# FFN 0's gate and up-projection by seven products of block sums in place of eight of blocks

## The chip, the cores and the metric

The kernel runs on one core of one Trainium2 chip. The metric is the device time of one execution in microseconds (us), taken as the median of several runs. Beside it stands one profiled execution, from which every row of the profile comes.

## The reference

Two layers work on 512 latent tokens and 256 context tokens of width 1024. Each layer is a mixer (layer 0: grouped-query attention, layer 1: a bidirectional Mamba-2 scan) and a gated feed-forward network (FFN) with a width-3 convolution over positions on its gate:

```python
def conv_ffn(h, w_up, conv_w, conv_b, w_down):
    g, u = jnp.split(h @ w_up, 2, axis=-1)     # h (.., 1024), w_up (1024, 2 x 2816)
    g = dwconv_centred(g, conv_w, conv_b)      # over positions, width 3
    return (jax.nn.silu(g) * u) @ w_down       # w_down (2816, 1024)
```

In layer 0 this runs for both streams, 512 + 256 tokens, with the same weights. The input `h` is the RMS-normed stream with a scale and a shift, and the result enters the stream through a gate; scale, shift and gate are linear maps of SiLU of the condition vectors (the "modulation"). All is in f32.

## The kernel before

Activations lie transposed: features on the 128 partitions, tokens along the free axis. The 1024 input features are eight K tiles, the 2816 hidden features are 22 tiles f = 0 to 21. Every f32 operand of a large product is split into two fp32r parts, high and low (`split`: ScalarE casts the high part, VectorE, here DVE, subtracts for the low part, L85 and L87), and each product is three matmuls: weight high by activation high (L105), weight high by activation low (L106), weight low by activation high (L108). All three come from `mm3`.

FFN 0 is `ffn(g, 0, ...)`. For each f, `up(f)` computes the gate's tile with `gemm(f)` and the up tile with `gemm(22 + f)`. A `gemm` loads one weight tile of 128 x 1024 (`load_w`: a DMA on SyncE's queue into `wst`, then the split into `wh` and `wl`; all of these are tiles of the ring `t4`, ten buffers), and runs, for the latent stream with 512 columns and then for the context stream with 256, eight K tiles by three matmuls into one PSUM tile of two banks (`S`, two buffers). From the gate's PSUM, ScalarE makes `cv` (L833), DVE adds the two neighbouring taps (L837 and L838, for each stream), ScalarE applies SiLU (L839). DVE multiplies it with the up tile's PSUM into `hd` (L848), and `split` makes `hdh` and `hdl`. These are tiles of the ring `t3`, here 24 buffers.

The down-projection comes in flushes of two f each (`flush`, the first and the last of three): for each of the eight output tiles m, `down` accumulates the f's of the flush for both streams in two PSUM banks (four buffers of one bank), and DVE adds the result to the residual stream X (L784, once with 512 and once with 256 columns). The flush of a group is recorded after the first `up` of the next group.

Between these steps FFN 0 carries the modulation of layer 1 and of its own output gate: `ada_dve` is a generator that `up` and `down` advance (`next(side)`), two or more steps for each f and one for each m of a flush. A step is one DVE multiply-and-sum of a 128 x 1024 tile (`junk`, L167) on a weight tile `wada` that is loaded on SyncE's queue. The first 24 tiles serve two steps, the last 32 one. The ring of `wada` has three buffers:

```python
w = g.t3p.tile([P, D], F32, tag="wada", bufs=3, name="wada")
nc.sync.dma_start(w, g.I["adaT"][(ch + 1 if layer else 0) * KT + m])
```

A scheduler orders the instructions of each engine when the program is built, by the data they need, the free buffers and a model of durations; on the chip every engine and SyncE's DMA queue run in that order. The steps of `ada_dve` are held in program order.

The high and low parts of h are separate tiles for each stream (`htiles`, 16 of 512 and 16 of 256 columns).

Of the kernel before, what the change touches and what calls it, by code (L numbers as in the profile page):

```python
# [15 lines left out]
D = 1024  # L16
KT = D // P
L = 512
C = 256
T = L + C  # L20
# [4 lines left out]
NFT = FF // P  # L25
# [54 lines left out]

def split(g, src, hi, lo, lo_engine="dve", pin=False):

    nc = g.nc
    keep = g.tc.keep_in_program_order if pin else lambda i: i
    keep(nc.scalar.copy(hi, src))  # L85
    eng = nc.vector if lo_engine == "dve" else nc.gpsimd
    keep(eng.tensor_tensor(lo, src, _r(hi), ALU.subtract))  # L87
# [12 lines left out]
def mm3(g, w, outs, first, last):  # L100

    wh, wl = w
    mm = g.nc.tensor.matmul
    for out, (ah, al) in outs:
        mm(out, wh, ah, start=first, stop=False)  # L105
        mm(out, wh, al, start=False, stop=False)  # L106
    for out, (ah, al) in outs:
        mm(out, wl, ah, start=False, stop=last)  # L108
# [44 lines left out]
def ada_dve(g):  # L153


    nc = g.nc
    cb = g.t3p.tile([P, 2 * D], F32, name="cb")
    nc.sync.dma_start(cb, g.I["cflat"].broadcast_to([P, 2 * D]))
    follow(g, nc.scalar.activation(cb, cb, AF.Silu))
    for layer, ch, nv in [(0, 5, 2)] + [(1, ch, 2 if ch < 2 else 1) for ch in range(6)]:  # L160
        md = g.mod[layer][ch]
        for m in range(KT):
            w = g.t3p.tile([P, D], F32, tag="wada", bufs=3, name="wada")
            nc.sync.dma_start(w, g.I["adaT"][(ch + 1 if layer else 0) * KT + m])
            for v in range(nv):
                junk = g.t3p.tile([P, D], F32, tag="junk", bufs=1, name="junk")
                g.tc.keep_in_program_order(nc.vector.scalar_tensor_tensor(  # L167
                    junk, w, 1.0, cb[:, v * D : (v + 1) * D], ALU.mult, ALU.mult, accum_out=md[:, m, v : v + 1]))
                yield
        modulation(g, md[:, :, :nv], layer, ch, 0, KT, nv)  # L170
# [5 lines left out]
class Fill:  # L176
# [6 lines left out]
    def add(self, gen):  # L183
        self.q.append(gen)
# [83 lines left out]
    return out  # L268


def htiles(g, n, name):
    return tuple(g.p.tile([P, n], F32R, tag=f"h{n}", bufs=16, name=f"{p}{name}") for p in ("hh", "hl"))


def modulated(g, hl, x, rs, a, b, layer, ca, cb, v, m, pool=False):
# [26 lines left out]
def S(g, name):  # L302
    return g.ps.tile([P, 1024], F32, tag="S", bufs=2, name=name)
# [6 lines left out]
class Norm:  # L310
# [2 lines left out]

    def __init__(self, g, layer, ca, cb, streams, name):
        self.g, self.a, self.name, self.streams = g, (layer, ca, cb), name, streams
        self.h = [[htiles(g, n, f"{name}{i}_{m}") for m in range(KT)] for i, (n, v) in enumerate(streams)]
        self.acc = {}

    def sq(self, seg, x, m):
# [59 lines left out]
def attention(g, fill, X, late):  # L379


    nc, I = g.nc, g.I
    S64 = slice(0, 64), slice(64, 128)
    Bk, Sb = (lambda name: Bank(g, name)), (lambda name: S(g, name))
    t2 = lambda name, dt=F32: g.t3p.tile([P, 512], dt, tag="t2", bufs=6, name=name)
    g.h = [[htiles(g, n, f"a{i}_{m}") for m in range(KT)] for i, n in enumerate((L, C))]
    hl, hc = g.h
    kn = g.par[:, PC["kn"] : PC["kn"] + 1]

# [28 lines left out]
    xs = [[X[:, m, c0:c1] for m in range(KT)] for c0, c1 in ((0, L), (L, T))]  # L418
# [23 lines left out]
    norm = rstd_rows(g, acc, L, g.ones[:, :1], D, "a", Bk)  # L442
# [3 lines left out]
    e = g.p.tile([P, 2 * KT], F32, name="silu")  # L446
# [8 lines left out]
    rsl, _, _ = next(norm)  # L455
# [12 lines left out]
    for m in range(KT):  # L468
# [37 lines left out]
    raw = [t3(g, f"raw{j}") for j in range(6)]  # L506
# [207 lines left out]
    odram = [g.dp.tile([P, T], F32, name=f"odram{p}") for p in range(6)]  # L714

    def osplit(p):
        hl_, hc_ = htiles(g, L, f"ol{p}"), htiles(g, C, f"oc{p}")
# [13 lines left out]
    m = pairs[0].maxima()  # L731
# [8 lines left out]
    for p in range(NH // 2):  # L740
        m = iter(())
        if p < 7:
# [3 lines left out]
            m = pairs[p + 1].maxima()  # L746
# [49 lines left out]
def ffn(g, layer, streams, x, h, first, nxt=None, side=iter(()), after=()):  # L796

    nc, I = g.nc, g.I  # L800
    ns = len(streams)
    tot = sum(n for n, _ in streams)
    off = [0, L]

    cw = [g.par[:, PC[f"fw{layer}{t}"] : PC[f"fw{layer}{t}"] + NFT] for t in range(3)]
    cb = g.par[:, PC[f"fb{layer}"] : PC[f"fb{layer}"] + NFT]
    whole = [[(i, 0, n) for i, (n, _) in enumerate(streams)]]

    def gemm(t):

        if t % NFT == 0:
            ps = first[t // NFT]
        else:
            w = load_w(g, I["wup"][layer, t])
            if t % NFT == 1:
                out = []
                for i in range(ns):
                    ps = Bank(g, "ps_up1")
                    for _ in gemm_in(g, [(ps, w)], h, (0, 0), [[s] for s in whole[0] if s[0] == i]):
                        pass  # L820
                    out.append((ps, [i]))
                return [(ps[:, : streams[i][0]], off[i], off[i] + streams[i][0], i) for ps, (i,) in out]
            ps = S(g, "ps_up")
            for _ in gemm_in(g, [(ps, w)], h, off, [[s] for s in whole[0]]):
                pass
        return [(ps[:, :tot], 0, tot, None)]

    def up(f):
        pg = gemm(f)
        cv = t3(g, "cv", n=tot)  # L830
        w0, w1, w2 = (c[:, f : f + 1] for c in cw)
        for ps, a, b, _ in pg:
            nc.scalar.activation(cv[:, a:b], ps, AF.Identity, scale=w1, bias=cb[:, f : f + 1])  # L833
        for i in range(ns):
            a, b = off[i], off[i] + streams[i][0]
            ps, o = next((ps, o) for ps, o, e, j in pg if j in (None, i))
            nc.vector.scalar_tensor_tensor(cv[:, a + 1 : b], ps[:, a - o : b - o - 1], w0, cv[:, a + 1 : b], ALU.mult, ALU.add)  # L837
            nc.vector.scalar_tensor_tensor(cv[:, a : b - 1], ps[:, a - o + 1 : b - o], w2, cv[:, a : b - 1], ALU.mult, ALU.add)  # L838
# [4 lines left out]
        pu = gemm(NFT + f)  # L843
        for _ in range(some):
            next(side, None)
        hd = t3(g, "hd", n=tot)
# [32 lines left out]
def ssd(g, x, norm, wf, bg, close):  # L879


    nc, I, tc = g.nc, g.I, g.tc
    par = lambda name, j, rows=P: g.par[:rows, PC[name] + j : PC[name] + j + 1]
    h = norm.h
# [285 lines left out]
        prev = cur  # L1170


    xn = [[g.p.tile([P, C], F32, tag="h256", bufs=16, name=f"x{m}{i}") for i in range(2)] for m in range(KT)]
# [81 lines left out]
def body(nc, tc, I, out, dbg=None):  # L1255
# [3 lines left out]
    es = ExitStack()  # L1259
    pool = lambda n, st=es, **k: st.enter_context(tc.tile_pool(name=n, bufs=1, **k))  # L1260
    g.const, g.p = pool("const"), pool("p")
    g.ps = g.t3p = None
    phx, pha = ExitStack(), ExitStack()
    X = pool("x", phx).tile([P, KT, T], F32, name="X")
# [49 lines left out]
    first = first_tiles(g, wf, nrm, bg)  # L1314
    pha.close()
    phf = ExitStack()
    g.t3p, g.n3 = pool("pf", phf), 24


    def dump():  # L1320
# [13 lines left out]
        phf.close()  # L1334
        phx.close()

    x, nrm, first = ssd(g, x, nxt, wf, bg, close)
    phf = ExitStack()
    g.t3p, g.n3 = pool("pg", phf), 24
    if not (dbg and dbg.get("stage") == 3):  # L1340
# [105 lines left out]
```

## Time and profile before

| | |
|---|---|
| median of 3 runs | 1908.88 us (1906.4 to 1910.08) |
| profiled execution | 1914.7 us, its span 1912.9 us |
| mean granted TensorE clock | 0.994 |
| TensorE matmuls (PE) | 1876.5 us busy, 98% of the span |
| weight loads (PEld) | 1547.6 us, 81% |
| DVE | 1311.2 us, 69% |
| ScalarE (ACT) | 823.0 us, 43% |
| GpSimd (POOL) | 309.8 us, 16% |
| FFN 0's matmuls | about 418 to 1000 us of the span |

A row of a group names line, engine, operation, output and inputs with their shapes and the count; then the busy time in us and the mean ns of one; then the engine's idle time just ahead of these instructions and what ended it. A row of the timeline begins with the start and the length in us. Matmuls overlap: the time that one costs is the distance from its start to the next one's start, not its length. DVE's instructions overlap a little too.

### The profile page before, as it was taken

What the parts mean: (1) busy time and instruction counts of PE and PEld (TensorE: products, weight loads), DVE (VectorE), ACT (ScalarE), POOL (GpSimd) and SP (SyncE); (2) the same over time, 40 slices, a digit from 0 to 9 for tenths busy, and PEclk for the clock granted to TensorE, in tenths of its full rate; (3) what the DMA queues carried; (4) which work ended last, traced back from release to release, by engine and by line L of the source; (5) the groups of instructions that cost most, each with busy time, mean ns of one, the idle gap of its engine ahead of it and who ended that gap; (6) DMA issues with size and microseconds to landing.
All of it is one profiled execution on the core that took longest, in us unless ns stands there. A gap on an engine that the chain in (4) does not pass through costs nothing.

```text
span 1912.9 us, 27512 instructions
## 1 busy us (share of the span) xinstructions
PE 1876.5 (98%) x10834; PEld 1547.6 (81%) x10834; DVE 1311.2 (69%) x1943; ACT 823.0 (43%) x1426; POOL 309.8 (16%) x274
## 2 busy tenths in 40 slices
PE   9999999999999999999999999999999999999999
PEld 7866555678888888888888888888888878888887
DVE  5578778678877777444488777777888466565555
ACT  3634444255122222222266777776667352323331
POOL 2241111031000000000040344443434210000000
PEclk9989998999999999999999999999999999999999
DMA  9221332114434555221122443334443322323232
GB/s 337 78 89 45 113 112 95 34 45 166 132 122 132 174 188 166 66 67 60 62 89 87 121 118 115 126 113 133 120 138 115 91 77 86 102 88 110 88 100 88
DMA packets 73425, 210.02 MB, mean 110 GB/s; under 512 B 8912, under 2 KB 14416, under 8 KB 73168
## 3 DMA queue, kind: packets, MB, share of 16 engines
q1 hardware_dynamic: 73296, 208.26, 34.3%
q8 instruction: 85, 1.39, 0.3%
q14 instruction: 44, 0.36, 0.1%
HBM read 198.79 MB, written 6.82 MB: 107 GB/s over the span
## 4 chain that ended last, share of the span: by engine, by line
PE 79%; DVE 9%; issue 3%; ACT 2%; POOL 1%; DMA 1%; DVEq 0%; SPq 0%; POOLq 0%; ACTq 0%
PE ps_up L106 10%; PE ps_up L108 10%; PE ps_up L105 10%; PE ps_d L105 6%; PE ps_d L106 6%; PE ps_d L108 6%; PE ps_in L106 4%; PE ps_in L108 4%; PE ps_in L105 4%; PE ps_o L637 2%; PE ps_s L673 2%; PE ps_st L1033 2%; DVE ht L281 1%; PE ps_wo L108 1%; PE ps_wo L105 1%
## 5 line engine op out<-in xcount | busy, mean ns | idle before, releaser
L87 DVE TENSOR_TENSOR wl<-wst,wh 128x1024 fp32r<-128x1024 f32 x205 | 254.5, 1242 | 244.9 <-PE ps_up L106 137.7
L85 ACT CAST wh<-wst 128x1024 fp32r<-128x1024 f32 x211 | 221.2, 1049 | 423.2 <-DMA wst<-in_wup 333.8
L106 PE MATMUL ps_up<-hlf,wh 128*128 128x512 f32 x1008 | 357.0, 354 | 0.0
L105 PE MATMUL ps_up<-hhf,wh 128*128 128x512 f32 x1008 | 356.9, 354 | 0.0
L108 PE MATMUL ps_up<-hhf,wl 128*128 128x512 f32 x1008 | 356.8, 354 | 0.0
L105 PEld LDWEIGHTS ps_up<-hhf,wh 128*128 128x128 f32 x1008 | 190.5, 189 | 26.5
L106 PEld LDWEIGHTS ps_up<-hlf,wh 128*128 128x128 f32 x1008 | 190.6, 189 | 26.4
L108 PEld LDWEIGHTS ps_up<-hhf,wl 128*128 128x128 f32 x1008 | 190.5, 189 | 26.4
L105 PE MATMUL ps_in<-hhs,wh 128*128 128x512 f32 (+1 forms) x560 | 204.4, 365 | 0.0
L106 PE MATMUL ps_in<-hls,wh 128*128 128x512 f32 (+1 forms) x560 | 199.4, 356 | 0.0
L108 PE MATMUL ps_in<-hhs,wl 128*128 128x512 f32 (+1 forms) x560 | 198.7, 355 | 0.0
L105 PE MATMUL ps_d<-hdh,wh 128*128 128x512 f32 (+1 forms) x568 | 193.6, 343 | 1.4 <-DVE X L784 1.2
L108 PE MATMUL ps_d<-hdh,wl 128*128 128x512 f32 (+1 forms) x568 | 193.5, 341 | 0.0
L106 PE MATMUL ps_d<-hdl,wh 128*128 128x512 f32 (+1 forms) x568 | 193.0, 340 | 0.3 <-DVE hdl L87 0.3
L784 DVE SCALAR_TENSOR_TENSOR X<-ps_d,mod,X 128x512 f32<-128x512 f32 (+1 forms) x224 | 124.6, 583 | 36.9 <-PE ps_d L108 36.6
L106 PEld LDWEIGHTS ps_d<-hdl,wh 128*128 128x128 f32 x568 | 106.6, 188 | 14.8 <-DVE hdl L87 0.7
L105 PEld LDWEIGHTS ps_d<-hdh,wh 128*128 128x128 f32 x568 | 106.3, 188 | 14.8 <-DVE X L784 1.4
L105 PEld LDWEIGHTS ps_in<-hhs,wh 128*128 128x128 f32 x560 | 105.9, 189 | 15.1 <-issue 1.2
L108 PEld LDWEIGHTS ps_in<-hhs,wl 128*128 128x128 f32 x560 | 105.8, 189 | 14.8
L108 PEld LDWEIGHTS ps_d<-hdh,wl 128*128 128x128 f32 x568 | 106.7, 188 | 13.1
L106 PEld LDWEIGHTS ps_in<-hls,wh 128*128 128x128 f32 x560 | 106.0, 189 | 13.2
L676 ACT ACTIVATE pr<-ps_s 128x1024 f32<-128x1024 f32 x56 | 57.2, 1021 | 110.6 <-PE ps_s L675 109.6
(340 smaller groups left out, 3547.3 us busy)
## 6 DMA issues: line engine op xcount, KB each, us to landing
wst<-in_wup SPq DMA_DIRECT2D x88, 512.0 KB, 3.6
wada<-in_adaT SPq DMA_DIRECT2D x56, 512.0 KB, 3.9
wst<-in_win SPq DMA_DIRECT2D x48, 512.0 KB, 3.7
wst<-in_wdown SPq DMA_DIRECT2D x44, 512.0 KB, 3.6
E<-ad SPq DMA_DIRECT2D x64, 256.0 KB, 6.8
wada<-in_adaB SPq DMA_DIRECT2D x24, 512.0 KB, 4.6
ec<-ead SPq DMA_DIRECT2D x64, 128.0 KB, 5.0
wst<-in_wout SPq DMA_DIRECT2D x16, 512.0 KB, 3.6
```

The lines of the kernel that those rows point to most:

```text
L85: keep(nc.scalar.copy(hi, src))
L87: keep(eng.tensor_tensor(lo, src, _r(hi), ALU.subtract))
L105: mm(out, wh, ah, start=first, stop=False)
L106: mm(out, wh, al, start=False, stop=False)
L108: mm(out, wl, ah, start=False, stop=last)
L281: nc.vector.scalar_tensor_tensor(t[:, c0:c1], ap, g.moda[layer][ca][:, m, v : v + 1], rs[:, c0:c1], ALU.mult, ALU.mult)
L637: nc.tensor.matmul(po[S64[e], :n], v, pr[:, 512 * e + off : 512 * e + off + n], start=first, stop=last)
L673: nc.tensor.matmul(outs[e], a[S64[e], k], b[S64[e], q], start=i == 0, stop=False)
L676: nc.scalar.activation(pr, ps, AF.Exp)
L784: nc.vector.scalar_tensor_tensor(ap, o[:, c0:c1], gate[:, m, v : v + 1], ap, ALU.mult, ALU.add)
L1033: nc.tensor.matmul(ps[:, d * 256 : (d + 1) * 256], Bt[:, t * P : (t + 1) * P], xw[d][t], start=t == ts[0], stop=t == ts[-1])
```

## The change

Only the tiles f = 4 to 21 of FFN 0 and K tiles 0 to 3 of their eight are computed in another way. Take the product of weights (gate and up, that is two output blocks; two K blocks of two K tiles each) and activations (the same K blocks; two halves of 384 tokens of the 768): two by two blocks by two by two blocks. The eight products of blocks become seven products of sums of blocks, the scheme of Strassen in Winograd's form, with K tiles 4 to 7 added as before:

- `sums()`, once, ahead of f = 2: 20 adds and subtractions of 128 x 384 on GpSimd make four sums T0 to T3 of the activations, and four splits follow.
- `both(f)` takes the place of `gemm(f)` and `gemm(22 + f)`. It loads both weight tiles, makes four sums of 128 x 256 of the weights on GpSimd (`wss`), and splits gate (1024 columns), sums (1024) and the second to fourth quarter of up (768). Then come the products, each of 384 columns; `a` and `e` are the two banks of the first PSUM tile, `b` and `r` those of the second.
- The results are combined outside PSUM: four ScalarE copies (`p1`, `p5`, `x1`, `r0`), four DVE adds from PSUM (`u` twice, `r1`, `x0`) and four GpSimd adds in SBUF, all of 128 x 384. The gate (`raw`) and the up tile (`x`) then stand in SBUF, where `up` reads them.

To make room in SBUF, the ring `t3` of FFN 0 has 16 buffers instead of 24, and `wada` two instead of three. The parts of h for both streams lie in one tile of 768 columns (`g.H`), in a pool of its own that is closed before layer 1's scan ends; `hpair` gives the slices.

```diff
-            w = g.t3p.tile([P, D], F32, tag="wada", bufs=3, name="wada")
+            w = g.t3p.tile([P, D], F32, tag="wada", bufs=2, name="wada")
...
+def hpair(g, m, i=0):
+
+    if g.H:
+        return tuple(t[:, i * L : (L, T)[i]] for t in g.H[2 * m : 2 * m + 2])
+    return htiles(g, L, f"f{m}")
...
+    HT = tot // 2
+    half = lambda i: slice(i * HT, (i + 1) * HT)
+    fast = range(4, NFT) if ns > 1 else ()
+    hi_lo = lambda m, i: tuple(t[:, half(i)] for t in g.H[2 * m : 2 * m + 2])
...
+    def both(f):
+
+        sg, su, ss = t4(g, "wst"), t4(g, "wst"), g.t3p.tile([P, 1024], F32, tag="ws", bufs=3, name="wss")
+        for st, t in ((sg, f), (su, NFT + f)):
+            nc.sync.dma_start(st, I["wup"][layer, t])
+        wg, wu = ((t4(g, "wh", F32R), t4(g, "wl", F32R)) for _ in range(2))
+        ws = tuple(g.t3p.tile([P, 1024], F32R, tag="ws", bufs=3, name=n) for n in ("wsh", "wsl"))
+        q = lambda t, i: t[:, 256 * i : 256 * i + 256]
+        for out, x, y, op in ((0, q(su, 0), q(su, 1), ALU.add), (2, q(sg, 0), q(su, 0), ALU.subtract),
+                              (1, q(ss, 0), q(sg, 0), ALU.subtract), (3, q(sg, 1), q(ss, 1), ALU.subtract)):
+            nc.gpsimd.tensor_tensor(q(ss, out), x, y, op)
+        split(g, sg, *wg)
+        split(g, ss, *ws)
+        split(g, su[:, 256:], wu[0][:, 256:], wu[1][:, 256:])
+        pg, pu = S(g, "ps_up"), S(g, "ps_up")
+        a, e, b, r = pg[:, :HT], pg[:, 512 : 512 + HT], pu[:, :HT], pu[:, 512 : 512 + HT]
...
+        product(a, (wg, 0, B(0, 0)))
+        product(e, (ws, 0, Ts[0]))
+        product(r, (wu, 4, rest(1)))
+        nc.scalar.copy(p1, a)
+        nc.scalar.copy(p5, e)
+        product(b, (ws, 2, Ts[1]))
+        nc.scalar.copy(x1, r)
+        add(nc.gpsimd, x1, x1, p5)
+        product(a, (wg, 2, B(2, 0)), (wg, 4, rest(0)))
+        add(nc.vector, u, p1, b)
+        add(nc.gpsimd, p5, p5, u)
+        product(b, (ws, 4, Ts[2]))
+        nc.scalar.copy(r0, a)
+        add(nc.gpsimd, r0, r0, p1)
+        add(nc.vector, u, u, b)
+        add(nc.gpsimd, x1, x1, u)
+        product(e, (ws, 6, B(2, 1)), (wg, 4, rest(1)))
+        product(b, (wu, 2, Ts[3]), (wu, 4, rest(0)))
+        add(nc.vector, r1, p5, e)
+        add(nc.vector, x0, u, b)
+        return raw, x
...
-    g.t3p, g.n3 = pool("pf", phf), 24
+    g.t3p, g.n3 = pool("pf", phf), 16
```

In this text "product 7" is `product(b, (ws, 4, Ts[2]))`, six matmuls; the two after it have 18 each. Line numbers of the changed program are 85 and 87 for the splits, 898 for the adds and 167 for the modulation steps.

More of the change, by code (lines that the diff above doesn't have):

```diff
@@ L385, in attention @@
     t2 = lambda name, dt=F32: g.t3p.tile([P, 512], dt, tag="t2", bufs=6, name=name)
-    g.h = [[htiles(g, n, f"a{i}_{m}") for m in range(KT)] for i, n in enumerate((L, C))]
+    g.h = [[hpair(g, m, i) for m in range(KT)] for i in range(2)]
     hl, hc = g.h
@@ L826, in gemm, with sums, less @@
         return [(ps[:, :tot], 0, tot, None)]
-    def up(f):
-        pg = gemm(f)
+    HT = tot // 2
+    half = lambda i: slice(i * HT, (i + 1) * HT)
+    fast = range(4, NFT) if ns > 1 else ()
+    hi_lo = lambda m, i: tuple(t[:, half(i)] for t in g.H[2 * m : 2 * m + 2])
+    def sums():
+        eng, f32 = nc.gpsimd, lambda m, i: tuple(_r(t) for t in hi_lo(m, i))
+        def less(x, y):
+            d, e = (t3(g, n, n=HT) for n in "de")
+            eng.tensor_tensor(d, x[0], y[0], ALU.subtract)
+            eng.tensor_tensor(e, x[1], y[1], ALU.subtract)
+            return d, e, ALU.add
+        T = [t3(g, f"T{i}", n=tot) for i in range(4)]
+        for j in range(2):
+            t1, t2, t3_, t4_ = (t[:, half(j)] for t in T)
+            for out, (x, y, op) in ((t1, less(f32(j, 1), f32(j, 0))), (t3_, less(f32(2 + j, 1), f32(j, 1)))):
+                eng.tensor_tensor(out, x, y, op)
+            for out, (h, l), y in ((t2, f32(2 + j, 1), t1), (t4_, f32(2 + j, 0), t2)):
+                eng.tensor_tensor(out, h, y, ALU.subtract)
+                eng.tensor_tensor(out, out, l, ALU.add)
+        out = []
+        for i, t in enumerate(T):
+            h, l = (g.t3p.tile([P, tot], F32R, name=f"T{c}{i}") for c in "hl")
+            split(g, t, h, l)
+            out.append([(h[:, half(j)], l[:, half(j)]) for j in range(2)])
+        return out
@@ L830, in up @@
+    def up(f):
+        if ns > 1 and f == 2:
+            Ts.extend(sums())
+        if f in fast:
+            raw, x = both(f)
+            pg = [(raw, 0, tot, None)]
+        else:
+            pg = gemm(f)
         cv = t3(g, "cv", n=tot)
@@ L1170, in ssd @@
         prev = cur
-    xn = [[g.p.tile([P, C], F32, tag="h256", bufs=16, name=f"x{m}{i}") for i in range(2)] for m in range(KT)]
+    close_h()
+    xn = [[g.hp.tile([P, C], F32, name=f"x{m}{i}") for i in range(2)] for m in range(KT)]
     for m in range(KT):
@@ L1261, in body @@
     g.const, g.p = pool("const"), pool("p")
+    phh = ExitStack()
+    hp = pool("h", phh, side="right")
+    g.H = [hp.tile([P, T], F32R, name=f"h{i}") for i in range(2 * KT)]
     g.ps = g.t3p = None
```

32 lines of the change are left out of this document (25 added, 7 removed).

## The prediction

> **What bounds the kernel now.** I read the page's busy times first, then its chain, then who TensorE waited for, then windows over FFN 0.
>
> ```profile
> PE 1876.5 (98%) x10834; PEld 1547.6 (81%) x10834; DVE 1311.2 (69%) x1943; ACT 823.0 (43%) x1426; POOL 309.8 (16%) x274
> PE 79%; DVE 9%; issue 3%; ACT 2%; POOL 1%; DMA 1%; DVEq 0%; SPq 0%; POOLq 0%; ACTq 0%
> PE ps_d L106 <- DVE hdl L87: 0.3, 1, 0.3
> PE ps_d L105 <- ACT hdh L85: 0.2, 1, 0.2
> 500.00:600.00 100.00, 100.00 (x579) 88.20 (x578) 73.89 (x116) 22.16 (x23) 0.00 (x0) 1.00 0.41 133
> 600.00:700.00 100.00, 100.00 (x578) 88.25 (x577) 76.16 (x124) 22.00 (x24) 0.00 (x0) 1.00 0.57 179
> 700.00:800.00 100.00, 100.00 (x577) 88.21 (x577) 65.66 (x101) 23.63 (x25) 0.00 (x0) 1.00 0.38 122
> 800.00:900.00 100.00, 100.00 (x579) 88.27 (x578) 49.23 (x69) 22.90 (x24) 0.00 (x0) 1.00 0.21 65
> L167 DVE SCALAR_TENSOR_TENSOR junk<-wada,cb x80: 1208/1215/1227, 455.4 to 763.0; 128x1024 f32<-128x1024 f32 x80
> ```
>
> Matmuls end the kernel. The two wait rows are all that TensorE waited between 450 and 970 us (FFN 0): half a microsecond. In the windows (columns: stretch, length, then busy time and count of PE, PEld, DVE, ACT and POOL, granted clock, DMA) PE is full, DVE is the next engine, and it comes in two stages: about 75 us of every 100, then 49. The difference is the 80 modulation steps (`junk`, L167; last row), vector work for layer 1 spread over the first half of FFN 0, up to 763 us. So a matmul removed in FFN 0 shortens the kernel one for one as long as DVE keeps up, and DVE is what to count.
>
> **What goes: matmul time.** Two 512-column stretches and one 256-column stretch of one tile, 24 matmuls each, begin and end at these rows:
>
> ```profile
> 640.14 0.40 PE L105 MATMUL ps_up<-hhf,wh 128*128 128x512 f32 x1
> 645.61 0.28 PE L105 MATMUL ps_up<-hhf,wh 128*128 128x256 f32 x1
> 648.48 0.40 PE L105 MATMUL ps_up<-hhf,wh 128*128 128x512 f32 x1
> ```
>
> 5.47/24 = 0.2279 us for 512 columns, 2.87/24 = 0.1196 for 256. A 384-column matmul isn't in the trace; it lies between them, and the midpoint is 0.1737 (by the 256-column row's rate per column it would be 0.1794, by the 512's 0.1709). One feature tile f (gate and up) takes 48 of each now: 16.68 us. Changed, it takes 7 products x 2 K tiles x 3 plus 4 K tiles x 2 x 2 halves x 3 = 90 matmuls: 15.63. Tiles f = 4 to 21 do this: 18 x 1.05 = **18.8 us less** (9.6 to 23.4 by the two rates, the 384 dearer or cheaper).
>
> **What comes: vector work.** I count per pair of tiles, with the down-projection ("flush": 48 and 48 matmuls) that follows every second tile. The same split stands 50 us apart in two pairs, which is 3 x 16.68 = 50.0; changed, the matmuls of a pair take 31.26 + 16.68 = 47.95.
>
> ```profile
> 598.67 1.23 DVE L87 TENSOR_TENSOR wl<-wst,wh 128x1024 fp32r<-128x1024 f32 x1 [5.25 <-PE ps_up L106]
> 648.62 1.22 DVE L87 TENSOR_TENSOR wl<-wst,wh 128x1024 fp32r<-128x1024 f32 x1 [5.25 <-PE ps_up L106]
> 599.82 0.74 DVE L837 SCALAR_TENSOR_TENSOR cv<-ps_up,par,cv 128x511 f32<-128x511 f32 x1
> 602.17 1.22 DVE L167 SCALAR_TENSOR_TENSOR junk<-wada,cb 128x1024 f32<-128x1024 f32 x1
> 612.08 1.14 DVE L784 SCALAR_TENSOR_TENSOR X<-ps_d,mod,X 128x512 f32<-128x512 f32 x2
> 623.06 1.14 DVE L784 SCALAR_TENSOR_TENSOR X<-ps_d,mod,X 128x512 f32<-128x512 f32 x2
> 626.49 1.21 DVE L167 SCALAR_TENSOR_TENSOR junk<-wada,cb 128x1024 f32<-128x1024 f32 x1
> 627.62 1.22 DVE L87 TENSOR_TENSOR wl<-wst,wh 128x1024 fp32r<-128x1024 f32 x1
> L87 DVE TENSOR_TENSOR hdl<-hd,hdh 128x768 fp32r<-128x768 f32 x10 | 9.5, 950 | 0.0
> L784 DVE SCALAR_TENSOR_TENSOR X<-ps_d,mod,X 128x256 f32<-128x256 f32 x40 | 19.0, 474 | 0.8 <-PE ps_d L108 0.8
> L1100 DVE TENSOR_TENSOR ec<-ec,ps_yo 128x512 f32<-128x512 f32 x20 | 13.2, 680 | 3.6 <-PE ps_yo L1098 3.6
> L833 ACT ACTIVATE cv<-ps_up,par 128x768 f32<-128x768 f32 x20 | 19.8, 992 | 35.0 <-PE ps_up L108 35.0
> L85 ACT CAST wh<-wst 128x1024 fp32r<-128x1024 f32 x69 | 72.5, 1050 | 252.9 <-DMA wst<-in_wup 207.2 <-DMA wst<-in_wdown 18.1 <-DVE cv L838 12.8
> ```
>
> Prices of one in a queue, start to start: a 1024 op 1.13 (626.49 to 627.62), a 768 op 0.08 under its 0.95, so 0.87; the four conv taps 2.35 (599.82 to 602.17); in a flush one X pair and one modulation step 10.98/5 = 2.20 (612.08 to 623.06). A 384-column add with one PSUM operand is between 0.47 and 0.68: 0.58. So each tile adds 4 x 0.58 plus one more 768 split, 3.2 us, and a pair 6.4. DVE's load per pair goes from 37.5 (75%) to 43.9 of 47.95 with the modulation steps (92%), and from 24.6 to 31 (65%) without. By sum alone it still fits. By order it doesn't, and this is what I forecast from.
>
> In the changed program's issue order DVE stands, in each second tile, at `u += b` (it needs product 7), and behind it comes everything up to the next tile's weights. For the flushes after f = 5, 7 and 11, counting from product 7's end: u 0.6; the split of the weight sums, which waits for matmuls that free its buffer (1.04) and a ScalarE copy (1.05), ends at 3.3; `r1` 0.6, next gate split 1.13, taps 2.35, `x0` 0.6: 8.0; two steps, `hd` and `hdl`: 12.0; eight X pairs with eight steps 17.6, and 0.3 for finished modulations: 29.9; only then the split of the next tile's up weights, 0.87: 30.8. TensorE meanwhile has products of 18 and 18 matmuls (6.3), what is left of the flush (14.6) and 32 matmuls of the next tile that the scheduler put between (5.6): 26.4. It waits 4.4 us. Behind that stands another split (1.13) ahead of the next `u`, whose weights are loaded late (below): 0.4 to 2 more. I take 5.5 for each. The cover that hides this now is the order: a weight tile is used for 8.3 us by one matrix, its successor split long before; in the change gate, up and sums of one tile are all due within 2 us of its start.
>
> After f = 9 three splits stand behind all the steps. From product 7's end: `u` and a down-weight split 1.8; `r1` when the next product ends, 3.7; ScalarE's `cv` 1.0, taps, `x0` and a first step: 8.9. Then nine steps, eight X pairs, `hd` and `hdl` 20.5, two splits 2.3, and the modulation loads:
>
> ```profile
> wada<-in_adaT SPq DMA_DIRECT2D x56, 512.0 KB, 3.9
> SPq L164 <- DVE junk L167: 168.9, 51, 7.2
> ```
>
> With two `wada` buffers for three a load may start only when the step two before has ended, and lands 3.9 later, 4.3 with issue and signals (an estimate). From here every step has its own tile, so there is one each (1.13 + 4.3)/2 = 2.7 us, not 2.2: 3.4 over the seven that this holds. Sum 35.1, less 1.1 because six matmuls run ahead of the last split: 34.0. TensorE has work for 23.3 (6.3 + 16.5 of the flush + 0.5). It waits 10.7. (The second row shows that SyncE's queue already stands in these waits for 169 us; the up-weights queued behind them are what comes late above.) After f = 13 four steps are left: 2.2 by the same count. For the pairs after that the count leaves 0.5 each, 2 in all.
>
> ScalarE gets four 384 copies a tile and half a cast more, some 2.5 us in 24 where it was busy for 22 of 100: nothing, its idle time hides it. GpSimd was idle here and gets four 256 sums and four 384 adds a tile:
>
> ```profile
> L330 POOL TENSOR_TENSOR sqf<-sqf,sqf 128x256 f32<-128x256 f32 x15 | 11.2, 744 | 115.7 <-ACT sqf L325 114.7 <-ACT rsy L241 0.4
> L1101 POOL TENSOR_TENSOR ec<-ec 128x512 f32<-128x512 f32 x12 | 18.4, 1535 | 110.3 <-DVE ec L1100 110.3
> L87 DVE TENSOR_TENSOR wl<-wst,wh 128x1024 fp32r<-128x1024 f32 x31 | 37.9, 1222 | 53.7 <-PE ps_up L106 24.3 <-ACT wh L85 22.3 <-issue 7.1
> L87 DVE TENSOR_TENSOR wl<-wst,wh 128x1024 fp32r<-128x1024 f32 x32 | 41.2, 1286 | 6.7 <-ACT wh L85 6.7
> 1100.00:1400.00 300.00, 298.54 (x1765) 259.07 (x1765) 218.12 (x250) 210.41 (x467) 127.84 (x110) 1.00 0.39 116
> ```
>
> 0.74 and 1.1 each, 7.4 us of a tile's 24. Its `p5 += u` must end before the second `u` add: 1.1 in the 3.1 us that 18 matmuls cover, so hidden. The 20 sums of h (some 22 us) have two tiles of 16.7 before their first reader; their four DVE splits (3.5) fall where the count still closes. What GpSimd costs DVE is in the last three rows: a 1024 split takes 1.222 in FFN 0, where GpSimd is idle, and 1.286 where it is busy for 128 of 300 us. I take 0.2 us of DVE per us of GpSimd that falls into the stretches, 3 us for the kernel; bounds 0 (no overlap) and 8. The GPSIMD Engine Reference of the Trainium skill, § 8 Key points, says that GpSimd shares its SBUF interfaces with VectorE and contends with its instructions of two SBUF inputs; the trace agrees (1.286 for 1.222). By it the splits, the steps and `hd`, with two SBUF inputs each, and GpSimd's adds would slow each other in every pair.
>
> Sum: -18.8 + 3 x 5.5 + 10.7 + 2.2 + 2 + 3 = **+15.6 us**. The profiled execution took 1914.7 with a span of 1912.9, 0.3% over the median of 1908.88; on the median it gives 1924.5.
>
> **The rivals.**
> *DVE keeps up, faster.* Place: the next tile's up split after f = 5, 7, 9, 11. It decides when DVE reaches that split within the 26.4 us (23.3 after f = 9) that TensorE has. For it: 92% is below 100, and DVE stood idle a quarter of the time. Against: DVE runs in order, and its idle time lies ahead of product 7, not behind. Then only the 2.2, the 2 and half the contention stay: -13, 1896.
> *Stalls half as long, no change.* If the waits overlap better than in my count: -18.8 + 15 + 3 = -1, 1908.
> *The clock.* The largest idle stretch of TensorE before a row in attention is 1.79 us, and the clock stayed; elsewhere it fell to 0.57 for 7 us:
>
> ```profile
> 104.92 0.66 PE L253 MATMUL rsTq<-cst,rbq 128*128 128x128 f32 x4 [1.79 <-DVE rbq L247]
> 295.00:302.00 7.00, 7.00 (x32) 4.62 (x31) 4.14 (x7) 1.02 (x1) 0.00 (x0) 0.57 0.00 0
> ```
>
> If a wait of 4 us or more does what happened at 295, each of four costs up to 7 x 0.43 = 3 us: +12, 1937. TensorE: Matmul & The Clock Gate of the Trainium skill, Part 1, halves the clock after an idle window of about 3.4 us. The four waits here would pass it; no row of this trace has one that long.
> *GpSimd and DVE slow each other throughout.* By the counts and prices above GpSimd gets some 15 us a pair. At 0.3 us of DVE for each (an estimate, above the 0.2 taken), over nine pairs and half of it on the path, that is 20, of which 3 stand in the forecast: the sum is +33, near 1942.
> *The products don't save.* At 0.1794 for a 384 the gain shrinks to 9.6 and the sum grows by 9: 1934. It is inside the forecast's range, and its chance in the forecast's.
>
> **How the numbers follow.** Forecast 1924 (chance 0.50), clock 0.13, contention 0.12, no change 0.09, DVE keeps up 0.16. The forecast's own range, stalls a third smaller or larger, is 1914 to 1935. The whole range leaves out the lowest part of the faster case and the highest of clock and contention: 1898 to 1946. No change is within 0.2% (3.8 us), about what a measurement of this kernel tells apart. Faster 0.16, same 0.09, slower 0.75.
>
> **What would show it.** Right: 384-column matmuls 0.17 us apart; TensorE waiting for `wl` and `wsl` (L87) and for `u` (L898) for some 30 us in all, most after f = 9 and none after about 790 us; DVE over 85% until then; pairs of 53 us early, 48 late. Wrong: PE full in these windows and FFN 0 shorter by 15 us or more; or waits behind GpSimd, or stalls that go on after the modulation steps have ended.

## The result: 4.5% slower, and the profile after

The changed kernel takes 1993.62 us (median of four runs, 1990.31 to 1995.53) against 1907.97 for the kernel before: 1.0446 times, 95% interval 1.0427 to 1.0466. That is some 85 us more; forecast were 16 more, and at most 37. The profiled execution took 1994.97 us with a span of 1993.2, 80.3 over the span of before.

The busy times and the chain of the changed kernel's page:

```profile
PE 1902.3 (95%) x10726; PEld 1585.9 (80%) x10726; DVE 1374.2 (69%) x2037; ACT 871.6 (44%) x1520; POOL 478.2 (24%) x438
PE 50%; DVE 11%; issue 4%; DMA 4%; POOL 3%; ACT 2%; SPq 0%; POOLq 0%; DVEq 0%; ACTq 0%
```

There are 108 matmuls fewer, and yet TensorE is busy for 25.8 us longer (1902.3 for 1876.5): single matmuls have become slower. And TensorE's share of the chain has fallen from 79 to 50%: it waits. Both are seen in windows cut at the ends of the flushes, one pair of tiles with its flush in each (columns as in the prediction; the first row is a pair of the kernel before, the others are of the changed kernel, from the flush of f = 3 and 4 on):

```profile
574.30:624.30 50.00, 50.00 (x291) 44.12 (x290) 37.65 (x61) 11.57 (x12) 0.00 (x0) 1.00 0.41 127
```
```profile
590.50:646.80 56.30, 50.82 (x277) 47.23 (x276) 43.93 (x70) 16.63 (x22) 16.22 (x16) 0.97 0.36 112
646.80:708.70 61.90, 49.31 (x255) 44.44 (x254) 41.85 (x67) 15.44 (x20) 17.57 (x16) 0.94 0.47 148
708.70:773.00 64.30, 55.81 (x297) 51.57 (x296) 49.00 (x72) 17.39 (x24) 18.53 (x16) 0.95 0.49 151
773.00:834.40 61.40, 50.99 (x261) 46.60 (x260) 41.39 (x67) 15.34 (x20) 17.55 (x16) 0.92 0.38 122
834.40:885.50 51.10, 49.20 (x278) 46.28 (x278) 30.55 (x45) 16.46 (x23) 18.30 (x20) 1.00 0.24 73
885.50:934.20 48.70, 48.55 (x278) 46.27 (x277) 29.86 (x45) 16.65 (x23) 13.99 (x17) 1.00 0.22 66
```

A pair took 50.0 us. Now it takes 56 to 64 while the modulation steps run (the last one starts at 823.5 us), with a granted clock of 0.92 to 0.97, and 48.7 with a full TensorE from 885.5 us on. DVE is busy for 67 to 78% of the first four windows. The gain of the products is there; the first half of FFN 0 loses several times as much. By the start times of the matmuls, FFN 0 takes 608.0 us from the first of `ps_up` to the last of `ps_d`, for 538.9: 69.1 of the 80.3 lie there.

Whom TensorE waits for, first from 590.5 to 885.5 us, then one answer ahead of it (440 to 590.5) and one behind it (885.5 to 1040); columns: us in total, times, longest:

```profile
PE ps_up L108 <- DVE wl L87: 15.9, 4, 6.1
PE ps_d L105 <- DVE X L791: 9.0, 6, 3.0
PE ps_up L105 <- DVE gr L898: 4.5, 4, 1.4
PE ps_up L105 <- ACT gr L914: 2.9, 3, 1.0
PE ps_d L105 <- ACT hdh L85: 2.5, 3, 1.0
PE ps_up L105 <- ACT p L906: 2.1, 3, 1.0
PE ps_up L105 <- DVE hd L898: 2.0, 2, 1.0
...
PE ps_d L105 <- ACT wh L85: 4.6, 1, 4.6
PE ps_d L105 <- DVE X L791: 2.8, 1, 2.8
PE ps_up L105 <- DVE gr L898: 2.1, 1, 2.1
PE ps_up L105 <- ACT p L906: 1.0, 1, 1.0
...
PE ps_d L105 <- ACT hdh L85: 5.6, 1, 5.6
```

The middle stretch sums to 38.9 us, the stretch before it to 10.5, the last flush to 5.6: 55 in all, where it was half a microsecond.

**One wait followed back.** The longest, after the flush of f = 7 and 8: TensorE's matmul, then DVE's rows and SyncE's queue ahead of it.

```profile
715.24 0.69 PE L108 MATMUL ps_up<-h,wl 128*128 128x384 f32 x1 [6.12 <-DVE wl L87]
...
707.35 1.23 DVE L167 SCALAR_TENSOR_TENSOR junk<-wada,cb 128x1024 f32<-128x1024 f32 x1 [0.32 <-DMA wada<-in_adaT]
708.50 1.80 DVE L791 SCALAR_TENSOR_TENSOR X<-ps_d,mod,X 128x512 f32<-128x512 f32 x3
710.37 1.23 DVE L167 SCALAR_TENSOR_TENSOR junk<-wada,cb 128x1024 f32<-128x1024 f32 x1
712.82 1.23 DVE L167 SCALAR_TENSOR_TENSOR junk<-wada,cb 128x1024 f32<-128x1024 f32 x1 [0.82 <-DMA wada<-in_adaT]
713.97 1.22 DVE L87 TENSOR_TENSOR wl<-wst,wh 128x1024 fp32r<-128x1024 f32 x1
715.10 1.22 DVE L87 TENSOR_TENSOR wsl<-wss,wsh 128x1024 fp32r<-128x1024 f32 x1
...
701.12 13.29 SPq L164 DMA_DIRECT2D wada<-in_adaT  x6
714.46 0.90 SPq L875 DMA_DIRECT2D wst<-in_wup  x2
```

The next tile's gate split (713.97) is the first thing behind the last modulation step of this flush. The six steps from 699.86 to 712.82 stand 2.6 us apart on average, and ahead of four of them DVE waited for a `wada` tile to land, by 0.3 to 1.1 us. TensorE starts when the gate split has ended (713.97 + 1.22 = 715.19). And the weights of the tile after that have only now been asked for (714.46), because the queue stood for 13.29 us in the loads of `wada`. This is the mechanism that was forecast, at the place that was forecast.

**The clock behind a wait.** The same wait and a shorter one (2.08 us, ended at 550.41), in windows:

```profile
711.00:714.00 3.00, 0.00 (x0) 0.00 (x0) 2.18 (x6) 0.00 (x0) 0.00 (x0) 1.00 0.62 191
714.00:721.00 7.00, 5.76 (x18) 5.76 (x19) 3.51 (x6) 1.89 (x4) 0.03 (x1) 0.51 0.71 253
721.00:724.00 3.00, 3.00 (x19) 3.00 (x18) 2.88 (x3) 1.23 (x2) 3.00 (x3) 1.00 0.00 0
...
550.00:554.00 4.00, 3.59 (x12) 3.59 (x13) 2.84 (x6) 1.96 (x2) 0.00 (x0) 0.57 0.28 110
```

The granted clock is half for 7 us around the end of the wait of 6.12 and for 3.5 us behind that of 2.08. Ten waits of FFN 0, of 2.08 to 6.12 us, do this, six times for some 3.4 us and four times for some 6.8. The sum of (1 - granted clock) over windows of 4 us from 440 to 1076 us is 23.8 us; in the kernel before it is 0.0 there.

**Slower matmuls.** The same code in layer 1's FFN, the first and the last of 96 matmuls in a row, of the kernel before and of the changed one:

```profile
1656.77 0.40 PE L105 MATMUL ps_up<-hhf,wh 128*128 128x512 f32 x1
1678.35 0.39 PE L108 MATMUL ps_up<-hhf,wl 128*128 128x512 f32 x1
```
```profile
1666.70 0.39 PE L105 MATMUL ps_up<-hhf,wh 128*128 128x512 f32 x1
1688.77 0.39 PE L108 MATMUL ps_up<-hhf,wl 128*128 128x512 f32 x1
```

21.58/95 = 0.2272 us from start to start, and 22.07/95 = 0.2323. Nothing of the seven products is near. What differs is where h lies: at the lower end of SBUF (7 to 56 KB of a partition) before, in a pool at the upper end (180 to 229 KB) after, with the weight tiles at 56 to 97 and at 7 to 48 KB.

### The profile page after: what moved, and what is told of

The parts are those of the page before. It is cut to its first block, busy times and chain, and to the rows that moved or that the text cites. A ratio compares the mean times of both kernels' runs of the same rounds, so it can differ in the third digit from the quotient of the medians.

```text
span 1993.2 us, 27713 instructions
## 1 busy us (share of the span) xinstructions
PE 1902.3 (95%) x10726; PEld 1585.9 (80%) x10726; DVE 1374.2 (69%) x2037; ACT 871.6 (44%) x1520; POOL 478.2 (24%) x438
## 4 chain that ended last, share of the span: by engine, by line
PE 50%; DVE 11%; issue 4%; DMA 4%; POOL 3%; ACT 2%; SPq 0%; POOLq 0%; DVEq 0%; ACTq 0%
PE ps_up L108 6%; PE ps_up L105 6%; PE ps_up L106 6%; PE ps_in L108 4%; PE ps_in L106 4%; PE ps_in L105 4%; PE ps_d L105 4%; PE ps_d L106 4%; PE ps_d L108 4%; POOL wss L881 2%; DVE wl L87 2%; DVE junk L167 2%; PE ps_st L1137 2%; DMA wada<-in_adaT 1%; DMA wst<-in_wup 1%
## 5 line engine op out<-in xcount | busy, mean ns | idle before, releaser
L87 DVE TENSOR_TENSOR wl<-wst,wh 128x1024 fp32r<-128x1024 f32 (+1 forms) x205 | 254.6, 1244 | 139.2 <-ACT wh L85 71.4
L85 ACT CAST wh<-wst 128x1024 fp32r<-128x1024 f32 (+1 forms) x211 | 216.9, 1030 | 305.5 <-DMA wst<-in_wup 192.6
L105 PE MATMUL ps_in<-h,wh 128*128 128x512 f32 (+1 forms) x560 | 205.8, 367 | 0.1
L106 PE MATMUL ps_in<-h,wh 128*128 128x512 f32 (+1 forms) x560 | 200.8, 359 | 0.0
L108 PE MATMUL ps_in<-h,wl 128*128 128x512 f32 (+1 forms) x560 | 200.4, 358 | 0.0
L108 PE MATMUL ps_up<-h,wl 128*128 128x384 f32 (+2 forms) x456 | 157.6, 346 | 15.9 <-DVE wl L87 15.9
L105 PE MATMUL ps_up<-h,wh 128*128 128x384 f32 (+2 forms) x456 | 158.2, 347 | 11.7 <-DVE gr L898 6.6
L106 PE MATMUL ps_up<-h,wh 128*128 128x384 f32 (+2 forms) x456 | 157.1, 344 | 0.0
L105 PEld LDWEIGHTS ps_d<-hdh,wh 128*128 128x128 f32 x568 | 108.7, 194 | 43.9 <-DVE X L791 16.0
L106 PE MATMUL ps_up<-hlf,wh 128*128 128x512 f32 x336 | 132.6, 395 | 0.0
L108 PE MATMUL ps_up<-hhf,wl 128*128 128x512 f32 x336 | 132.6, 395 | 0.0
L105 PE MATMUL ps_up<-hhf,wh 128*128 128x512 f32 x336 | 132.4, 394 | 0.0
L105 PEld LDWEIGHTS ps_in<-h,wh 128*128 128x128 f32 x560 | 105.5, 188 | 16.4 <-issue 1.2
L106 PEld LDWEIGHTS ps_in<-h,wh 128*128 128x128 f32 x560 | 105.5, 188 | 14.7
L167 DVE SCALAR_TENSOR_TENSOR junk<-wada,cb 128x1024 f32<-128x1024 f32 x80 | 101.9, 1273 | 6.8 <-DMA wada<-in_adaT 5.7
```

The lines of the kernel that those rows point to most:

```text
L167: g.tc.keep_in_program_order(nc.vector.scalar_tensor_tensor(junk, w, 1.0, cb[:, v * D : (v + 1) * D], ALU.mult, ALU.mult, accum_out=md[:, ...
```

## The experiments

The kernel before, timed beside each of them, took 1908 to 1909 us.

| kernel | median, us | ratio to before (95%) |
|---|---|---|
| before, h at the upper end | 1924.41 | 1.0058 to 1.0104 |
| changed, ends of SBUF exchanged | 1992.82 | 1.0407 to 1.0473 |
| changed, eight products | 1929.93 | 1.0083 to 1.0133 |
| changed, steps out of the flushes | 1958.05 | 1.0227 to 1.0291 |
| changed, h next to the weights | 1988.44 | 1.0389 to 1.0432 |
| steps out, sums earlier | 1954.95 | 1.0213 to 1.0271 |
| steps out, adds on DVE | 1955.93 | 1.0231 to 1.0267 |
| all mends together | 1954.41 | 1.0226 to 1.0260 |
| changed, 64 steps left out | 1940.76 | 1.0149 to 1.0179 |
| seven products for f = 14 to 20 | 1911.11 | 1.0002 to 1.0029 |
| seven products for f = 11 to 20 | 1918.33 | 1.0031 to 1.0061 |

**The place of h.** First the kernel before with h at the upper end:

```diff
-    return tuple(g.p.tile([P, n], F32R, tag=f"h{n}", ...
+    return tuple(g.hp.tile([P, n], F32R, tag=f"h{n}", ...
...
     g.const, g.p = pool("const"), pool("p")
+    g.hp = pool("h", side="right")
```

> The kernel before with one edit: the tiles of h (high and low parts, the moving operand of the large products) come from a pool at the upper end of SBUF (180 to 229 KB of a partition) instead of the lower end (7 to 56 KB); their neighbours move down by as much. Theory A (place): TensorE's distance from matmul to matmul depends on where the moving operand lies; in the changed kernel's second FFN, whose code is the same, 512-column matmuls on h stand 0.2325 us apart for 0.2272 before, while those on hd tiles keep their distance. Then this kernel shows 0.2325 there too, and with some 3360 such matmuls of 512 columns and 1600 of 256 it takes 15 to 20 us more: 1923 to 1928. Rival (the joint 768-column tiles, or traffic of the changed kernel, or the chip's clock on that day): 0.2272 stays and the time is 1908.

It took 1924.41, 15 us more; by the start times in the profiles, 8.1 us more in FFN 0, 3.2 from there to the last of layer 1's projections, and 5.2 from the second FFN's first matmul to the end. The rows of its second FFN give 22.08/95 = 0.2324:

```profile
1662.94 0.40 PE L105 MATMUL ps_up<-hhf,wh 128*128 128x512 f32 x1
1685.02 0.39 PE L108 MATMUL ps_up<-hhf,wl 128*128 128x512 f32 x1
```

So it is the place, not the joint tile: in this kernel each stream has tiles of its own. The counterpart exchanges the two ends in the changed kernel (h from 7 KB up, weights at 188 to 229 KB):

```diff
-    g.const, g.p = pool("const"), pool("p")
+    g.const = pool("const")
...
-    hp = pool("h", phh, side="right")
+    hp = pool("h", phh)
+    g.p = pool("p", side="right")      # and x, pa, pf, pg, pt too
```

> The changed kernel with the two ends of SBUF exchanged: h from 7 KB up, all else from the upper end down; the order of instructions on every engine is the same. Theory A (place): 512-column matmuls on h at 0.227 to 0.228 again and 384-column ones at 0.172 for 0.1755 to 0.177; 15 to 20 us less: 1974 to 1979, with the waits in FFN 0 as they were. Rival: 1993, distances unchanged.

No gain in time: 1992.82. The expectation was wrong, and the rows say how: 22.17/95 = 0.2334 with h at the low end, where 0.227 to 0.228 was expected.

```profile
1663.42 0.39 PE L105 MATMUL ps_up<-hhf,wh 128*128 128x512 f32 x1
1685.59 0.39 PE L108 MATMUL ps_up<-hhf,wl 128*128 128x512 f32 x1
```

Not "high is slow", then. In both slow kernels h and the weights lie at opposite ends. (Theory A held in its direction only for the 384-column matmuls on h: 0.1737 from start to start for 0.1756 in the changed kernel.) A third layout puts h directly above the weights (weights 7 to 48, h 49 to 98 KB), the rest from the upper end down, again with the same order of instructions:

```diff
-    hp = pool("h", phh, side="right")
+    hp = pool("h", phh)                # x, pa, pf, pg, pt on the right
```

> The changed kernel, order of instructions the same, with h directly above the weight ring (weights 7 to 48 KB, h 49 to 98 KB) and everything else from the upper end down. Theory A, revised (the distance between matmuls grows when weights and moving operand lie far apart in SBUF: h at the upper end with weights at the lower took 0.2325 a 512, h at the lower end with weights at the upper 0.2333, hd within 30 to 90 KB of the weights 0.227 to 0.229): 512-column matmuls on h 0.227 to 0.228, 384-column ones on h near 0.172, and those of the second FFN's hd, now 130 KB and more away, 0.232; in sum some 14 us less: 1976 to 1982. Rival (the joint tile, or the alignment of the rows): 0.2325 and 1993.

```profile
1661.45 0.39 PE L105 MATMUL ps_up<-hhf,wh 128*128 128x512 f32 x1
1683.19 0.39 PE L108 MATMUL ps_up<-hhf,wl 128*128 128x512 f32 x1
```

21.74/95 = 0.2288, and the 384-column matmuls on h stand 0.1736 apart for 0.1756 (means over more than 1,000 distances each). The down-projection of that FFN, whose hd tiles now lie at 180 to 229 KB, went from 0.2291 to 0.2322 (470 pairs). The revised theory held in its direction on both; the time fell by 5 us, not by 14, to 1988.44, and its interval just touches that of the changed kernel. FFN 0 itself became no shorter, 610.0 us for 608.0 by the start times: the gain lies in the stages behind it. For 512 columns far apart is slow, in all five layouts that were run (the kernels with seven products from f = 14 or 11 on have weights at 188 to 229 and h at 138 to 188 KB: 0.2267 in the second FFN). For 384 columns it isn't so: 0.1737 with h low and the weights high is as short as 0.1736 with both side by side. From which distance on, or whether it is a border between parts of SBUF, no run tells.

**The room alone.** The changed kernel without the seven products:

```diff
-    fast = range(4, NFT) if ns > 1 else ()
+    fast = ()
...
-        if ns > 1 and f == 2:
+        if fast and f == 2:
```

> The changed kernel with the eight products for every f: no sums, no GpSimd adds, but the joint tiles of h at the upper end, two wada buffers and the ring of 16. Theory B (the vector work of the seven products, in DVE's order, makes the waits, and each wait of over 2 us costs TensorE about 2 us more of slow clock): no wait over 1 us in FFN 0, no slow clock there, only theory A's slower distance is left: 1923 to 1930. Rival (the room that was made: two wada buffers and 16 ring buffers hold DVE and SyncE's queue up): waits of 20 us or more in FFN 0's first half, 1945 or more.

1929.93, at the upper end of theory B's range: no wait over 0.3 us in FFN 0's pairs, no slow clock there. Two `wada` buffers and a ring of 16 cost nothing by themselves (FFN 0 takes 545.8 us for 547.0 in the kernel with h at the upper end); what the third buffer would be worth beside the seven products was not run. It is 5.5 us over the kernel with h at the upper end, and these lie at the seam behind the scan, which takes 122.7 us from the last projection's matmul to the second FFN's first for 117.3; one row of the waits there is new, in this kernel and in the changed one, and a stretch of slow clock stands behind it (3.4 us here, 6.8 in the changed one):

```profile
PE ps_y L1211 <- DVE E L1186: 3.0, 2, 1.8
```

Why DVE makes `E` later there was not followed up. So the products account for 1993.6 - 1929.9 = 64 us; FFN 0 alone is 62.2 longer with them by the start times.

**The steps.** Out of the flushes, two at each place of `up` from f = 4 on:

```diff
-        some = (2, 2, 2, 3)[f] if ns > 1 and f < 4 else 1
+        some = (2, 2, 2, 3)[f] if ns > 1 and f < 4 else 2
...
-        return down(..., order, norm, side=side)
+        return down(..., order, norm)
```

> The changed kernel with the 80 modulation steps taken out of the flushes: from f = 4 on two at each of the two places in up, none in the flushes, so that they end near f = 19 instead of f = 13. Theory B: X pairs and the next tile's splits no longer stand behind steps; of the waits of 38 us behind flushes 5 to 13 and the slow clock that follows them (about 14 us) most goes: 1940 to 1960. Rival (the chains of one tile, product to DVE to GpSimd to DVE to product, make the waits by themselves): 1980 or more, with waits in every pair up to f = 19.

1958.05: 36 us less, as theory B said. Two of its pairs, and the wait that leads now:

```profile
640.90:691.40 50.50, 48.80 (x277) 45.61 (x276) 39.35 (x61) 16.42 (x23) 15.64 (x16) 1.00 0.34 105
691.40:741.20 49.80, 48.32 (x275) 45.19 (x274) 39.34 (x63) 16.46 (x23) 15.31 (x17) 1.00 0.38 117
```
```profile
PE ps_up L105 <- ACT p L906: 13.2, 8, 1.9
...
776.26 0.83 ACT L85 CAST hdh<-hd 128x768 fp32r<-128x768 f32 x1 [1.10 <-DVE hd L952]
777.36 0.48 ACT L906 COPY p<-ps_up 128x384 f32<-128x384 f32 x1
777.90 0.44 PE L105 MATMUL ps_up<-h,wh 128*128 128x384 f32 x1 [1.91 <-ACT p L906]
```

Pairs of 50 for 62 and 64, with the same work in them but four steps fewer. The wait that leads now is one of ScalarE's order: its copy of a product (`p`) stands behind the cast of `hd`, and `hd` behind a step on DVE (774.13 to 775.35). The stronger form leaves 64 of the 80 steps and their loads out, so layer 1 runs without its modulation:

```diff
+        if layer:
+            nc.vector.memset(md[:, :, :nv], 0.0)
-        for m in range(KT):
+        for m in range(0 if layer else KT):
```

> The changed kernel with 64 of the 80 modulation steps and their loads left out (layer 1's modulation is set to zero; the 16 steps of layer 0's output gate stay). Theory B: nearly all waits in the middle of FFN 0 come from DVE being too full or too late beside these steps; without them only the waits at 480 to 550 us (9) and the last flush (5.6) with their slow clock are left, and FFN 0 gains what the products save, 18 x 1.07 = 19: 1925 to 1937. Rival (the products' own chain through ScalarE, DVE and GpSimd makes TensorE wait in every pair): 1950 or more.

```profile
600.00:700.00 100.00, 99.69 (x569) 95.17 (x569) 61.61 (x90) 34.09 (x45) 28.26 (x33) 1.00 0.22 64
```

Without steps the products run with a full TensorE from 600 us on, with 0.3 us of waits up to 940: the waits of the middle stretch need the steps or their loads. Its time, 1940.76, is outside the range given for theory B (to 1937) and under the rival's; 17.3 us of waits are left at the start of the sums and in the last flush, and its profile shows 6.8 us more of slow clock ahead of FFN 0 than that of the kernel with eight products, for which these runs give no cause.

**The start.** Why TensorE waited 4.62 us at 483 us is told by ScalarE's rows of the changed kernel:

```profile
474.55 1.81 ACT L85 CAST Th<-T 128x768 fp32r<-128x768 f32 x2 [1.61 <-POOL T L858]
478.99 0.83 ACT L85 CAST Th<-T 128x768 fp32r<-128x768 f32 x1 [2.62 <-POOL T L861]
481.74 0.83 ACT L85 CAST Th<-T 128x768 fp32r<-128x768 f32 x1 [1.92 <-POOL T L861]
482.47 1.04 ACT L85 CAST wh<-wst 128x1024 fp32r<-128x1024 f32 x1
```

The flush's weight cast (482.47) stands in order behind the casts of the sums of h, and these wait for GpSimd. In the kernel with even steps, the sums were begun at f = 1 and split at f = 3:

> The kernel with the even modulation steps (1958), and the block sums of h begun one tile earlier (f = 1) with their splits recorded two tiles later (f = 3). Theory C: the waits of 4.6 (for the flush's weight cast), 2.8 and 2.1 us at 480 to 550 us, with 5.7 of slow clock behind them, come from ScalarE and DVE standing in order behind the sums' splits, which wait for GpSimd; they go: 1943 to 1950. Rival (DVE is simply full there): the waits stay within 3 us of what they were, 1955 to 1960.

1954.95, whose interval overlaps that of 1958.05. The wait of 4.6 went, those of 2.8 and 2.1 became 1.1 and 1.5, and one of 4.8 us for the taps (`cv`) came in: neither theory is settled by the time.

**GpSimd.** In the kernel with even steps one of GpSimd's adds takes 2.00 us beside DVE's steps and another 1.01, begun while DVE waits; a DVE split right behind takes 1.54 us, beside the next add, for 1.22:

```profile
763.66 2.00 POOL L898 TENSOR_TENSOR hd<-hd,p 128x384 f32<-128x384 f32 x1
767.58 1.01 POOL L898 TENSOR_TENSOR gr<-gr,p 128x384 f32<-128x384 f32 x1
...
768.13 1.54 DVE L87 TENSOR_TENSOR wsl<-wss,wsh 128x1024 fp32r<-128x1024 f32 x1
```

The four adds were moved to DVE:

```diff
-        add(nc.gpsimd, x1, x1, p5)     # and p5 += u, r0 += p1, x1 += u
+        add(nc.vector, x1, x1, p5)
```

> The kernel with the even modulation steps (1958), and the four adds of each tile that GpSimd does behind the products moved to DVE (GpSimd keeps the sums of weights). Theory D: GpSimd's add takes 1.9 to 2.0 us beside DVE for 1.0 alone, DVE's split 1.5 for 1.22 beside GpSimd, and a chain of a tile goes through both; on DVE four adds take 4 x 0.5 and the waits of DVE for GpSimd go: 1958 or up to 15 us less. Rival (DVE's load decides: 85% of a pair, 4.4 us more a pair): more waits in every pair with steps, 1970 or more.

1955.93, no difference that these runs can tell; whether contention costs little, or as much as the adds on DVE, they don't say.

GpSimd has another part in the changed kernel. Its add `p5 += u` must end before DVE's second add into `u`, and GpSimd does it in order behind sums of weights (`wss`) that wait for loads: at 595.94 it begins four of them when a load has landed, at 601.76 the add, and at 602.81 DVE goes on. DVE's second adds in all:

```profile
L898 DVE TENSOR_TENSOR u<-u,ps_up 128x384 f32<-128x384 f32 x18 | 10.0, 554 | 56.6 <-POOL p L898 37.9 <-PE ps_up L108 18.7
```

DVE stood idle for 37.9 us for this add in the 18 tiles, 14.9 of them between 590.5 and 834.4 us. How much of that reached TensorE was not separated; the adds were moved only in the kernel with even steps.

**Better versions.** All mends in one (h near, sums earlier, four steps ahead of each tile, f = 21 by eight products):

> The changed kernel with all that the theories would mend: h next to the weights, sums earlier and their splits later, from f = 4 on four modulation steps ahead of each tile's products and none in the flushes, and the last tile f = 21 by eight products (the last flush waited 5.6 us for its hd). If waits fall under 10 us in FFN 0 and no slow clock is left: 1909 + 5 (the seam before the second FFN) - 17 + 10 = 1905 to 1912. Rival (the four steps in a row hold the chain of the tile before up): 1925 to 1945.

1954.41, above both ranges; the rival was nearer. TensorE waited 14.0 us for `X`, as it would if the steps in a row held the X pairs up. Then the seven products only where the steps have ended, or nearly:

> Seven products only for f = 14 to 20, where the modulation steps have ended; block sums at f = 11, their splits at f = 13; weights, h and the FFN rings next to each other at the upper end of SBUF. Expected: no waits beyond the kernel before's, 7 x 1.07 = 7.5 less matmul time, 5 more at the seam before the second FFN, distances between matmuls near before's: 1903 to 1909. Rival (the distances stay long): 1915 to 1922.

> As the one before, but seven products for f = 11 to 20, and the modulation steps two at each place of f = 4 to 10, so that they have ended by then (DVE's load of a pair of eight products goes from 75 to 85%). If DVE keeps up: 10 x 1.07 = 10.7 less, 1900 to 1906. Rival (at 85% DVE's order makes waits even with eight products): 1915 or more.

With f = 14 to 20 it took 1911.11, 0.15% over the kernel before and between the two ranges; pairs late in FFN 0 take 48.6 us for 49.9, but earlier ones 50.1 to 52.0 (their hd lies far from the weights, which may be a part of it), and the seam stays. From f = 11 with more steps ahead: 1918.33, with 9.2 us of waits for `X` (12 times): the rival. No version beat the kernel before.

## Why the prediction was wrong

The direction was right, and so was one mechanism, the next tile's splits behind X pairs and steps; the size was not, by 70 us. The forecast's sum was -18.8 for the matmuls, 31.4 for waits and 3 for GpSimd. Measured were -19.3 for the matmuls, 55 for waits, 23.8 for the slow clock, 15 for the place of h and 5.5 at the seam.

Right: the matmul time that goes. With the distances of the changed layout eight products of a tile take 24 x 2 x (0.2326 + 0.1190) = 16.88 us and 90 matmuls of 384 columns 90 x 0.1756 = 15.80, so 18 tiles save 19.3; forecast 18.8. Late pairs take 48.7; forecast 48. Right too: the next tile's splits behind X pairs and steps make TensorE wait until the steps end (15.9 us in four waits), the steps after f = 9 are slow (2.6 us apart between 699.86 and 712.82; forecast 2.7), and DVE's work for a pair is as counted (44.0 us on average in the four windows with steps; forecast 43.9). GpSimd's toll on DVE is nearer to the forecast's bound of 8 us than to its 3: the 80 steps take 1273 ns each for 1216 and 48 full splits of FFN 0 1287 for 1220, 7.8 us in all, not all of it where TensorE waits; the rival of contention throughout, 20 us, is not what happened.

Wrong, step by step:

- **The waits behind the flushes, 29.4 us forecast, 38.9 measured.** In the first five windows above, in order: 5.5 against 5.5, 12.4 against 5.5, 8.3 against 10.7 (the one behind f = 9), 10.4 against 5.5, and 1.9 against 2.2. The count followed only the next tile's weight splits, and only 15.9 of the 38.9 us are waits for these; that the first window's 5.5 agrees is luck, since 2.8 of it are for the split. The waits of 3.0, 1.9 and 3.0 for `X`, where DVE frees the down-projection's banks too late, and the 14.0 us for copies, casts and adds (`gr`, `p`, `hd`, `hdh`) are in no term of it. Nor was DVE full, as the signs to look for had it (over 85%): 67 to 78%, since it waited itself, for GpSimd's `p5 += u` among others, which the prediction called hidden.
- **The clock.** It was a rival with a price of at most 12 us, four waits of over 4 us, and a chance of 0.13. It should have been in the sum: ten waits of 2.08 us or more halved the clock, 23.8 us. The step that failed is the threshold of 4 us. It had one figure from below, the largest idle stretch of the profile that left the clock alone (1.79), and none from above: the slow clock from which the price was taken lasts from 290.8 to 301.0 us, and TensorE's longest idle stretch in 283 to 291 is 0.62 us. In the changed kernel a wait of 2.08 was enough; in the kernel with even steps three of five waits of 1.91 to 1.93 slowed the clock and two did not. At the seam waits of 1.22 and 1.78 us close to each other, ended at 1521.50 and 1523.68, were enough together. The Trainium skill (TensorE: Matmul & The Clock Gate, Part 1), on which the prediction drew for this, names an idle window of about 3.4 us. The same section says that the window runs freely, which agrees with waits of one length going both ways.
- **The sums of h**, "two tiles before their first reader", were costed at nothing. 10.5 us of waits lie in that stretch (440 to 590.5). For 4.6 of them the rows show why: the casts of the sums stand ahead of a flush's weight cast on ScalarE. What was left out is that order. For the others (2.8, 2.1 and 1.0) the cause isn't shown.
- **The last flush**, 5.6 us for `hdh`: the last tile's longer chain has no further tile to hide it. In the three kernels in which f = 21 has eight products no wait for `hdh` is longer than 0.8. No step of the prediction looked there.
- **The place of h.** Moving h to a pool at the other end of SBUF was read as making room and had no price. It costs 15 us by the run that does only this, in every stage that was read and multiplies h.
- **The seam**, 5.5 us: the prediction took everything outside FFN 0 as unchanged. Of these, 3.0 are the waits for `E`, and some 1.7 the slow clock behind them.

The account, in us: place of h 15, seam 5.5, products -19.3, waits in FFN 0 55, slow clock in FFN 0 23.8 (some of it falls into the ends of the waits). Together 80, of 80.3 in the profiles and some 85 in the medians. The sum is less exact than it looks: the slow clock ahead of FFN 0, which is in no term, costs 3.4 us less in the profile after than in that of before. How the waits of the middle stretch divide between X pairs behind steps, late weight loads and GpSimd was not separated; that they need the steps or their loads is shown, by the kernel without them.

## What to carry to other kernels

An algorithm that trades matmuls for vector adds is paid where the vector engine's order has room, not where its average has: here the same tiles gained 1.3 us a pair behind the modulation steps and lost 6 to 14 beside them. Count a wait of TensorE from about 2 us on with the slow clock behind it, as some waits of 1.9 us in these runs had it too, and look for every instruction that queues behind a new one on ScalarE, on DVE and on the DMA queue, the first and the last tile included. And a buffer that is only moved has a price to be measured.

## What the runs showed of the hardware

In layer 1's FFN, the distance between matmuls of 512 columns depended on where the weights and the moving operand lie in SBUF relative to each other: 0.2267 to 0.2292 us where they are neighbours, 0.2322 to 0.2334 where they are at opposite ends, about 2%, whichever of the two is above. For the 384 columns of FFN 0 it was 0.1756 with h above and the weights below, but 0.1737 the other way round and 0.1736 side by side. That was expected by nothing in the prediction, and its cause is open.
